# Moving three small bursts of matmuls in a hand-timed order: two steps of the fourth scan, and one projection of the decode tokens

## The chip, the cores and the metric

The kernel runs on one core of one Trainium2 chip. The metric is the device time of one execution in microseconds (us): three runs of the kernel before gave a median of 995.23 us (995.17 to 996.35). About 0.2%, or 2 us, is the least that a measurement of this kernel can tell from no change.

Five engines matter. TensorE (PE) multiplies matrices, VectorE (DVE) and ScalarE (ACT) work element by element, GpSimd (POOL) and SyncE (SP) mostly issue transfers. Each engine runs its own list of instructions in order and waits on semaphores for the others.

## The reference

One layer of a hybrid decoder step for one prompt of 2048 tokens and 8 decode tokens. The input is RMS-normalised and multiplied by a 1024 x 4096 matrix into eight groups of 512 columns: queries, keys, values and a gate for four retention heads, and query, forget gate, value and gate for four HGRN2 heads. Each head runs a decayed recurrence over the tokens:

```
o_inter = einsum('bhtd,bhdv->bhtv', qc * exp(b), S)          # b: cumulated log of the forget gate
A  = einsum('bhtd,bhsd,bhtsd->bhts', qc, kc, decay)           # HGRN2: the decay is per channel
o  = o_inter + einsum('bhts,bhsv->bhtv', A, vc)
S' = exp(bC) * S + einsum('bhsd,bhsv->bhdv', kc * exp(bC - b), vc)
```

Then comes a head-wise RMS norm, a SiLU gate, the output projection (1024 x 1024), the residual and a last RMS norm. Outputs are y for prompt and decode tokens and the final states.

## The kernel before, in words

**Units and products.** The input projection is cut into 24 units (`u` = 0 to 23, 12 for each half of the tokens); units 24 to 31 are the output projection. Unit `u` makes two rows of 128 columns for 1024 tokens: `u % 3` is 0 for HGRN2's forget gate and query (H in tile names), 1 for the two gates (G), 2 for retention's key and query (R). Each unit is a 2 x 2 block multiplication done with seven block products (`SLOTS`, line 876), each of 12 matmuls of 128 x 512: four blocks of the inner dimension by three terms of a high/low split. A product has a place in a time axis of 7 steps to a unit, and is issued in two halves of 6 matmuls. In a tile's name `aR`, `eR`, `bR` are the accumulators of a unit of kind R; `w11S` is a weight operand of unit 11, `x0T3h` the high part of the token operand T3 of the first half.

**The order is written out by hand.** `at(pos, f)` puts a function on a heap under a position; `after(d, f)` puts one `d` later than the function that is running. When everything is set up, the heap is emptied in order of position, and each function emits its instructions to all engines. So the position of an event sets the order on every engine at once, and nothing re-sorts it afterwards. The table `AT` holds the positions.

**The scan of an HGRN2 head** (`hgrn_rec`, line 1202) builds the 128 x 128 causal score blocks of eight chunks level by level. Each level needs k and q scaled by other products of forget gates. Its events for unit `u` stand at `7 u + AT["hgrn"][n] + AT["hd"][u // 3][n]`. There are eight scans, of units 0, 3, 6, ... 21; the second is that of unit 3, the fourth that of unit 9.

- First to third step, `s0`, `s1`, `s2` (`scores0`, `scores(1)`, `scores(3)`): a burst of 64 small matmuls by 32 x 16 (`small`, line 1269; the profile has two records for each), then on DVE `update` (kh and qth, lines 1234 and 1237), two masked copies (line 1275), and 0.35 later on ACT `keep` (copies of kh and qth, lines 1248 and 1249); 1.1 later another `update`. The change's title calls `s2` the second step and `s3` the third, counting from `s0` as zero.
- `s3` (`scores3`): two groups of small matmuls into the tiles p5 and p6 (lines 1321, 1330; both `plh` in the profile), a last `update`, and 0.3 later ten ACT copies into the score blocks `A`: four that read p5 (line 1340), two that read p6 (line 1342), four from `Ab` (line 1346).
- `k` (`kt`, line 1081): eight transposes of kh on TensorE (`pkh`, line 1085) into two tiles, and ACT copies of them (line 1091).

The small results of scans share one PSUM tag, `lv`, with two buffers (line 196), taken in turn: pl of `s1`, pl of `s2`, p5, p6, then the two tiles of the transposes. A new tile waits until all readers of the tile that had its buffer are done.

**The decode tokens.** For units 0 to 11, `dec_mm(u)` (line 804) multiplies the eight decode tokens with the raw weights of the unit (16 matmuls, `pdp`, line 809); `dec_copy` copies the result out on ACT. For a unit with `u % 3 == 0`, `dec_mm` stood at `7 u - 3.92`, for unit 3 just behind `s2` of the first scan.

**Next to the fourth scan** the token operands change from the first half to the second: `x_hi` on ACT (line 743) and `x_lo` on DVE (line 747) split what was loaded (`x1T1` and others), in two pieces each. `finish_block` of kind R rotates a block: two ACT copies (lines 1009, 1010, into `sw` or `big`) and three DVE operations (lines 1013, 1014, 750).

Of the kernel before, what the change touches and what calls it, by code (L numbers as in the profile page):

```python
# [48 lines left out]
def spooled(u):  # L49
    return u % 3 != 1 and u % 12 != 11  # L50
# [3 lines left out]
AT = {'wvl': (0.55, 0.6, 6.2, 6.6),  # L54
 's2': (0.4, 2.6),
 'vd': (9.4, 11.2),
 'hgrn': {'s0': 12.1,
          's1': 15.8,
          's2': 17.6,
          'load': 17.5,  # L60
          's3': 19.7,
          'k': 20.9,
# [79 lines left out]
         'fin': 25.2},  # L142
 'dh': ((12.15, 14.75), (17.55, 20.15), (27.15, 28.65)),
 'dhs': (-5.0, -2.2, -2.2, -1.5),
 'hd': ((0.0, 0.0, 0.0, 0.0), (0.0, 0.0, -0.5, -0.5), (0.0, 0.0, 0.0, 0.0), (0.3, 0.0, 0.0, 0.0),
        (0.0, 0.0, 0.0, 0.0), (0.0, 0.5, 0.0, 0.0), (0.0, 0.0, 0.0, 0.0), (0.0, 0.0, 0.0, 0.5)),
 'retL': {'load': 12.0,
          's': 11.55,
# [37 lines left out]
def step_kernel(ctx, tc, a, out):  # L186
# [31 lines left out]
    def at(pos, f):  # L218
        count[0] += 1
        heapq.heappush(ev, (pos, count[0], f))  # L220
# [550 lines left out]
    def w_load(u, n):  # L771
        R[u, n] = t_get([P, GW], f"r{u}{n}")
        row, kh = {"A11": (0, 0), "S3": (1, 0), "A22": (1, 1), "A12": (0, 1)}[n]
        sp.dma_start(R[u, n].rearrange("p (k t) -> p k t", k=4), w_src(u, row, kh))

    def w_s1(u):
        R[u, "S1"] = t_get([P, GW], f"r{u}S1")
        w_add(u, "S1", "S3", "A22", ALU.add)

    def w_s3(u):  # L780
        w_add(u, "S3", "A11", "S3", ALU.subtract)

    def w_s2(u):
        R[u, "S2"] = t_get([P, GW], f"r{u}S2")
        w_add(u, "S2", "A22", "S3", ALU.subtract)

    def w_s4(u):
        R[u, "S4"] = t_get([P, GW], f"r{u}S4")
        w_add(u, "S4", "A12", "S2", ALU.subtract)

    def w_split(u, n):
        w = W[u, n] = r_get(f"w{u}{n}")
        split_raw(w, R[u, n])
        t_done(R[u, n])
        if u < 12 and spooled(u):
            after(AT["late"], lambda: pool.dma_start(w_dram[u][W_NAMES.index(n)], w.bitcast(F32)))

    def w_reload(u, n):
        w = W[u, n] = r_get(f"w{u}{n}")
        sp.dma_start(w.bitcast(F32), w_dram[u - 12][W_NAMES.index(n)])  # L800
# [3 lines left out]
    def dec_mm(u):  # L804
        dec["pt"] = ps_o.tile([P, P], F32, tag="o", name=f"pdp{u}")
        for j in range(4):
            for g, n in enumerate(("A11", "A12", "S3", "A22")):
                at_ = 32 * (4 * (g % 2) + j)
                pe.matmul(
                    dec["pt"][32 * g : 32 * g + 32], xz[:, at_ : at_ + 32], R[u, n][:, j * P : (j + 1) * P],  # L810
                    start=(j == 0), stop=(j == 3),
                )

    def dec_copy(u):
        dec["e"] = t_get([P, P], f"de{u}")
        act.activation(dec["e"], dec["pt"], AF.Copy)

    def dec_sel(u):
        pt = ps_o.tile([P, 2, NB], F32, tag="o", name=f"pds{u}")
        pe.matmul(pt, dec["e"], sel16, start=True, stop=True)  # L820
        t_done(dec["e"])
        act.activation(draw[:, u % 3, :, u // 3], pt, AF.Copy)

    def prep_events(u):
        U = 7 * u
        w, d = AT["w"], AT["dec"]
        if 12 <= u < 24 and spooled(u):
            for name in W_NAMES:
                at(U + AT["re"][name], lambda name=name: w_reload(u, name))
            return  # L830
        for n, name in enumerate(("A11", "S3", "A22", "A12")):
            at(U + {0: -7.6, 1: -8.6}.get(u, AT["w24"][0] if u == 24 else w["load"] if u % 3 or u >= 12 else w["load0"]) + 0.5 * n, lambda name=name: w_load(u, name))
        if u < 12:
            if u == 3:
                at(AT["hgrn"]["s2"] + AT["hd"][0][2] + 0.01, lambda: dec_mm(u))
            else:
                at(U + d["mm" if u % 3 or not u else "mm0"], lambda: dec_mm(u))
            at(U + (-0.65 if u < 2 else d["copy" if u % 3 else "copy0"]), lambda: dec_copy(u))
            at(U + d["sel"], lambda: dec_sel(u))
        if u == 24:  # L840
            w = dict(w, **dict(zip(("S1", "S3", "S2", "S4"), AT["w24"][1:])))
        at(U + w["S1"], lambda: w_s1(u))
        at(U + w["S3"], lambda: w_s3(u))
        at(U + w["A11"], lambda: w_split(u, "A11"))
        at(U + w["S2"], lambda: w_s2(u))
        at(U + w["sS1"], lambda: w_split(u, "S1"))
        at(U + w["S4"], lambda: w_s4(u))
        at(U + w["sS2"], lambda: w_split(u, "S2"))
        at(U + w["sS4"], lambda: w_split(u, "S4"))
        at(U + w["sA12"], lambda: w_split(u, "A12"))  # L850
        at(U + w["sS3"], lambda: w_split(u, "S3"))
        at(U + w["sA22"], lambda: w_split(u, "A22"))
# [923 lines left out]
    for u in range(-6, 32):  # L1776
        U = 7 * u
        if u >= 0:
            prep_events(u)
        if 0 <= u < 24:  # L1780
            at(U - 0.01, lambda u=u: u_open(u))
        for n, sl in enumerate(SLOTS):
            s, d = sl[0], 0.5
            if is_last(u, n):
                s, d = (6.6, 0.2) if u < 0 else (7, 0.5)
            at(U + s, lambda u=u, n=n: product(u, n, 0))
            if u == 31 and is_last(u, n):
                at(U + s + 0.01, lambda u=u, n=n: evac(u, n))
            at(U + s + d, lambda u=u, n=n: product(u, n, 1))
            at(U + s + d + 0.01, lambda u=u, n=n: evac(u, n))  # L1790
# [164 lines left out]
```

## Time and profile before

| what | value |
|---|---|
| median of three runs | 995.23 us |
| the profiled execution | 994.56 us |
| its span from first to last instruction | 992.8 us |
| PE busy / DVE busy / ACT busy / POOL busy | 99% / 79% / 58% / 25% |
| granted TensorE clock | 0.999 |

In rows of the timeline the columns are: start from the span's beginning in us, time taken in us, engine, line, operation, output<-inputs, shapes, number of instructions merged into the row, and in brackets the idle time of the engine before it and what ended it. "issue" is idle time that no semaphore in the profile explains. A matmul's start is recorded and its end is modelled, so times on TensorE are best read from start to start. SP and POOL carry transfers; queue q8 carries instructions.

### The profile page before, as it was taken

The page shows a single profiled execution, that of the slowest core. Times are in us where ns is not written, and L with a number is a line of the kernel's source. Part 1 is how long each engine was busy: PE and PEld are TensorE (multiplying, and loading weights), DVE is VectorE, ACT ScalarE, POOL GpSimd, SP SyncE. Part 2 cuts the span into 40 slices and gives each one's busy share as a digit, 9 for nine tenths or more (in the row PEclk, how much of TensorE's full clock was granted, in tenths as well). Part 3 has the DMA queues.
Part 4 walks back from the last instruction along what each step waited for, and adds up shares of the span by engine and source line. Part 5 has one row for each costly group of instructions (what it writes and reads, how often), then busy time and mean ns, then how long its engine had stood idle before and what let it go on. Part 6 is the DMA issues. An engine that isn't in the chain of part 4 may idle for free. (4 is left out here: it accounts for less than half of the span.)

```text
span 992.8 us, 22960 instructions
## 1 busy us (share of the span) xinstructions
PE 978.9 (99%) x8831; PEld 815.9 (82%) x8831; DVE 779.6 (79%) x1355; ACT 575.5 (58%) x1348; POOL 252.5 (25%) x404
## 2 busy tenths in 40 slices
PE   9999999999999999999999999999999999999997
PEld 7788888888878887888888888888888878878886
DVE  6967696888778888878898766877867799867774
ACT  7855524856656664765885555456467577524332
POOL 1421231111332342232022222222237202312121
PEclk9999999999999999999999999999999999999999
DMA  9756669748868987784986993994996497784522
GB/s 310 239 182 245 223 218 360 291 154 301 261 194 279 300 284 266 269 273 159 354 277 187 320 307 121 317 303 130 317 333 215 156 362 275 244 267 156 212 85 85
DMA packets 121820, 244.05 MB, mean 246 GB/s; under 512 B 12600, under 2 KB 53184, under 8 KB 119024
## 3 DMA queue, kind: packets, MB, share of 16 engines
q1 hardware_dynamic: 98544, 164.69, 50.9%
q0 software_dynamic: 22880, 77.65, 21.1%
q8 instruction: 69, 1.13, 0.5%
q14 instruction: 39, 0.32, 0.1%
q10 hardware_dynamic: 288, 0.27, 0.1%
HBM read 155.97 MB, written 89.72 MB: 247 GB/s over the span
## 5 line engine op out<-in xcount | busy, mean ns | idle before, releaser
L1248 ACT ACTIVATE qh<-kh 128x1024 f32<-128x1024 f32 x24 | 25.5, 1062 | 46.3 <-DVE kh L1234 46.2
L1671 ACT ACTIVATE yj<-xro 128x512 f32<-128x512 f32 (+1 forms) x25 | 15.6, 624 | 60.3 <-DVE xro L750 42.7
L1234 DVE TENSOR_TENSOR kh<-kh,fph 128x512 f32<-128x512 f32 x48 | 33.0, 687 | 13.6 <-PE plh L1269 10.9
L1128 ACT ACTIVATE obh<-poh 128x128 f32<-128x128 f32 x64 | 16.9, 290 | 29.3 <-PE poh L1124 29.3
L1237 DVE TENSOR_TENSOR qth<-qth,fph 128x512 f32<-128x512 f32 x48 | 32.8, 683 | 0.0
L1128 ACT ACTIVATE obr<-por 128x128 f32<-128x128 f32 x64 | 16.8, 276 | 27.1 <-PE por L1124 27.1
L373 POOL TENSOR_TENSOR ms<-ms 128x2 f32<-128x2 f32 x8 | 10.0, 1255 | 86.5 <-ACT xn L369 86.5
L1689 DVE SCALAR_TENSOR_TENSOR xro<-xro,yms,fg 128x1024 f32<-128x1024 f32 (+1 forms) x16 | 20.0, 1247 | 13.5 <-POOL yms L1686 13.5
L1152 POOL DMA_DIRECT2D o_dram<-gtr x16 | 12.3, 769 | 67.5 <-DVE gtr L1149 20.8
L948 ACT ACTIVATE vo<-aV 128x512 f32<-128x512 f32 x12 | 7.1, 589 | 37.7 <-PE aV L918 37.7
L750 DVE TENSOR_TENSOR xro<-aO,xro 128x512 f32<-128x512 f32 (+1 forms) x33 | 22.2, 676 | 7.2 <-PE aO L918 7.1
L1152 POOL DMA_DIRECT2D o_dram<-gth x16 | 12.5, 778 | 57.5 <-DVE gth L1149 15.9
L265 POOL TENSOR_SCALAR orsh<-omsh 128x4 f32<-128x4 f32 x16 | 5.6, 347 | 83.3 <-ACT obh L1128 82.9
L1136 ACT ACTIVATE obh<-poh,orsh 128x128 f32<-128x128 f32 x64 | 18.2, 370 | 14.2 <-POOL orsh L266 14.2
L1115 DVE SCALAR_TENSOR_TENSOR sth<-sth,fph,puh 128x128 f32<-128x128 f32 x48 | 16.7, 347 | 10.3 <-PE poh L1124 7.8
L1122 PE MATMUL poh<-vh,A 128*128 128x128 f32 x128 | 24.0, 274 | 0.0
L1122 PE MATMUL por<-vr,A 128*128 128x128 f32 x128 | 24.0, 274 | 0.0
L1002 POOL DMA_DIRECT2D g_dram<-g x29 | 15.8, 546 | 27.8 <-DVE g L998 25.6
L1124 PE MATMUL por<-str,qr 128*128 128x128 f32 x112 | 21.8, 276 | 0.3 <-DVE str L1113 0.3
L369 ACT ACTIVATE xn<-xn 128x512 f32<-128x512 f32 x32 | 19.8, 622 | 3.5 <-DMA xn<-in_x_prompt 3.5
L1136 ACT ACTIVATE obr<-por,orsr 128x128 f32<-128x128 f32 x64 | 18.2, 368 | 6.1 <-POOL orsr L266 6.1
L1124 PE MATMUL poh<-sth,qth 128*128 128x128 f32 x112 | 21.7, 275 | 0.0
(1727 smaller groups left out, 3716.7 us busy)
## 6 DMA issues: line engine op xcount, KB each, us to landing
xn<-in_x_prompt SPq DMA_DIRECT2D x32, 256.0 KB, 4.4
v_dram<-vo SPq DMA_DIRECT2D x32, 256.0 KB, 2.4
xro<-in_x_prompt SPq DMA_DIRECT2D x16, 512.0 KB, 5.1
out_y_prompt<-xro POOLq DMA_DIRECT2D x15, 512.0 KB, 4.0
g_dram<-g POOLq DMA_DIRECT2D x29, 256.0 KB, 5.8
xr<-in_x_t SPq DMA_DIRECT2D x12, 512.0 KB, 6.2
vh<-v_dram SPq DMA_DIRECT2D x16, 256.0 KB, 8.8
gth<-g_dram SPq DMA_DIRECT2D x16, 256.0 KB, 6.7
```

The lines of the kernel that those rows point to most:

```text
L369: act.activation(r, r, AF.Square, accum_out=ms[:, 2 * h + j : 2 * h + j + 1])
L750: dve.tensor_tensor(o, x, y, op=ALU.add)
L1115: dve.scalar_tensor_tensor(dst, src, decay(c), pu[:, j], op0=ALU.mult, op1=ALU.add)
L1122: pe.matmul(po[:, j], s_ctx["A"][:, c], box["v"][g][:, j], start=True, stop=src is None)
L1124: pe.matmul(po[:, j], qcol(c), src, start=False, stop=True)
L1128: act.activation(ob[:, j], po[:, j], AF.Square, accum_out=ms[:, j : j + 1])
L1136: act.activation(ob[:, j], po[:, j], AF.Copy, scale=rs[:, j : j + 1])
L1152: after(AT["gate"]["tr"], lambda: pool.dma_start(o_dram[c0 : c0 + 4, ty, :, h].rearrange("c p t -> p c t"), gt.rearrange("p (c t) -> p c t ...
L1234: dve.tensor_tensor(kv[:, :, 0, :], kv[:, :, 0, :], two[:, :, 1:2].to_broadcast([P, nb, b]), op=ALU.mult)
L1237: dve.tensor_tensor(qv[:, :, 1, :], qv[:, :, 1, :], two[:, :, 0:1].to_broadcast([P, nb, b]), op=ALU.mult)
L1248: act.activation(kept_k, k, AF.Copy)
L1689: dve.scalar_tensor_tensor(x[:, cc], x[:, cc], ms[:, 0:1], fg[:, cc], op0=ALU.mult, op1=ALU.mult)
```

## The change

Three positions move. The second step (`s2`) of the fourth scan comes 1.0 later, its third (`s3`) 0.6 later, and `dec_mm` of unit 6 moves from 38.08 to 38.11, where `s2` of the second scan stands at 38.10. No instruction of computation is added or taken away; one wait instruction of TensorE (of 157) is no longer needed.

```diff
- 'hd': ((0.0, 0.0, 0.0, 0.0), (0.0, 0.0, -0.5, -0.5), (0.0, 0.0, 0.0, 0.0), (0.3, 0.0, 0.0, 0.0),
+ 'hd': ((0.0, 0.0, 0.0, 0.0), (0.0, 0.0, -0.5, -0.5), (0.0, 0.0, 0.0, 0.0), (0.3, 0.0, 1.0, 0.6),
         (0.0, 0.0, 0.0, 0.0), (0.0, 0.5, 0.0, 0.0), (0.0, 0.0, 0.0, 0.0), (0.0, 0.0, 0.0, 0.5)),
...
-            if u == 3:
-                at(AT["hgrn"]["s2"] + AT["hd"][0][2] + 0.01, lambda: dec_mm(u))
+            if u in (3, 6):
+                at(7 * (u - 3) + AT["hgrn"]["s2"] + AT["hd"][u // 3 - 1][2] + 0.01, lambda: dec_mm(u))
```

**Second scan, TensorE.** Before, from the last two `pdp` matmuls of unit 6 to the next product:

```order
L809 MATMUL pdp_3397<-r6S_3252,xz 32x128
L809 MATMUL pdp_3397<-r6A_3271,xz 32x128
L1269 MATMUL plh_3414<-fh_2585,qh_2625 32x16 x32
L1269 MATMUL plh_3414<-qth_2963,kh_2824 32x16 x32
L918 MATMUL aR_3234<-x0T2h,w5S_3231 128x512
```

Now, from the last matmul of the half product ahead to the first two of the 16 `pdp`:

```order
L918 MATMUL aR_3234<-x0T2h,w5S_3231 128x512
L1269 MATMUL plh_3397<-fh_2585,qh_2625 32x16 x32
L1269 MATMUL plh_3397<-qth_2963,kh_2824 32x16 x32
L809 MATMUL pdp_3464<-r6A_3241,xz 32x128
L809 MATMUL pdp_3464<-r6A_3282,xz 32x128
```

The two bursts, of 16 and 64 matmuls, have changed places; what stands before and behind them is the same.

**Fourth scan, TensorE, second step.** Before, at the end of product T2 of unit 11 (`aR`) and the start of product B22 (`eR`):

```order
L918 MATMUL aR_5391<-x0T2l,w11S_5388 128x512
L918 MATMUL aR_5391<-x0T2h,w11S_5388 128x512
L1269 MATMUL plh_5570<-fh_4744,qh_4783 32x16 x32
L1269 MATMUL plh_5570<-qth_5117,kh_4983 32x16 x32
L918 MATMUL eR_5419<-x0B22h,w11S_5416 128x512
```

Now, at the end of B22 and the start of B21 (`bR`):

```order
L918 MATMUL eR_5419<-x0B22l,w11S_5416 128x512
L918 MATMUL eR_5419<-x0B22h,w11S_5416 128x512
L1269 MATMUL plh_5586<-fh_4744,qh_4783 32x16 x32
L1269 MATMUL plh_5586<-qth_5117,kh_4983 32x16 x32
L918 MATMUL bR_5660<-x0B21h,w11A_5511 128x512
```

The burst has moved behind one product of 12 matmuls. In the same way p5 and p6, which stood between products B21 and T3 of unit 11, now stand in the middle of T3, 6 matmuls later; the transposes `pkh` keep their place behind T3, so 6 matmuls instead of 12 lie between p6 and them.

**Fourth scan, ACT.** Before, from the copy of qth that `keep` makes to the copies of the transposes:

```order
L1249 ACTIVATE fh_4744<-qth_5117 128x512
L1009 ACTIVATE sw_5676<-kr_5406 64x512
L1010 ACTIVATE sw_5676<-kr_5406 64x512
L743 ACTIVATE x1T1h<-x1T1l 128x1024
L1340 ACTIVATE A<-plh_5681 32x4x32 x4
L1342 ACTIVATE A<-plh_5682 64x4x64 x2
L1346 ACTIVATE A<-fh_4744 32x8x32 x4
L743 ACTIVATE x1T1h<-x1T1l 128x1024
L1009 ACTIVATE big<-kr_5406 64x512
L1010 ACTIVATE big<-kr_5406 64x512
L1091 ACTIVATE ksh_5762<-pkh_5757 128x512
```

Now:

```order
L1249 ACTIVATE fh_4744<-qth_5117 128x512
L1009 ACTIVATE sw_5674<-kr_5406 64x512
L1010 ACTIVATE sw_5674<-kr_5406 64x512
L743 ACTIVATE x1T1h<-x1T1l 128x1024 x2
L1009 ACTIVATE big<-kr_5406 64x512
L1010 ACTIVATE big<-kr_5406 64x512
L1340 ACTIVATE A<-plh_5692 32x4x32 x4
L1342 ACTIVATE A<-plh_5693 64x4x64 x2
L1346 ACTIVATE A<-fh_4744 32x8x32 x4
L1091 ACTIVATE ksh_5762<-pkh_5757 128x512
```

The ten copies into `A` now stand behind the second piece of `x1T1h` and a pair of rotation copies. On DVE the two additions into `kr` (from `eR` and from `bR`) now stand ahead of the scan's two updates instead of behind them. The orders of POOL and of SP are unchanged.

## Prediction

> **What bounds the kernel now.** I read the page first, then the waits of TensorE, then the timelines of the two stages that the change touches.
>
> ```profile
> span 992.8 us, 22960 instructions
> PE 978.9 (99%) x8831; PEld 815.9 (82%) x8831; DVE 779.6 (79%) x1355; ACT 575.5 (58%) x1348; POOL 252.5 (25%) x404
> ...
> PEclk9999999999999999999999999999999999999999
> ...
> q8 instruction: 69, 1.13, 0.5%
> ...
> PE plh L1269 <- issue: 3.4, 2, 2.5
> ```
>
> TensorE is busy from end to end at full clock, so the time is its list of instructions plus the holes in it. It waits 992.8 - 978.9 = 13.9 us in all; the largest single hole, 2.5 us, is inside a small burst and was ended by no semaphore ("issue"). An edit that moves bursts can save or cost time only by what a burst costs between products, and by holes.
>
> In the fourth scan before, TensorE has no hole:
>
> ```profile
> 475.01 0.39 PE L918 MATMUL aR<-x0T2h,w11S 128*128 128x512 f32 x1
> 475.33 0.70 PE L1269 MATMUL plh<-fh,qh 128*32 128x16 f32 x62
> ...
> 475.90 0.70 PE L1269 MATMUL plh<-qth,kh 128*32 128x16 f32 x62
> 476.53 0.50 PE L918 MATMUL eR<-x0B22h,w11S 128*128 128x512 f32 x1
> ...
> 479.18 0.39 PE L918 MATMUL eR<-x0B22h,w11S 128*128 128x512 f32 x1
> ...
> 481.90 0.39 PE L918 MATMUL bR<-x0B21h,w11A 128*128 128x512 f32 x1
> 482.22 0.46 PE L1321 MATMUL plh<-fh,qh 128*32 128x32 f32 x32
> 482.49 0.68 PE L1330 MATMUL plh<-qth,kh 128*32 128x64 f32 x32
> ...
> 485.97 1.03 PE L1085 MATMUL pkh<-ident,kh 128*128 128x128 f32 x8
> 486.76 0.48 PE L918 MATMUL aH<-x1B11h,w12A 128*128 128x512 f32 x1
> ```
>
> The last matmul of `eR` and that of `bR` are (481.90 - 479.18) / 12 = 0.227 us apart for each matmul. The burst of the second step takes 476.53 - 475.01 = 1.52 from product to product. The transposes (485.97) start with no gap.
>
> ACT in the same stretch:
>
> ```profile
> 478.90 1.06 ACT L1248 ACTIVATE qh<-kh 128x1024 f32<-128x1024 f32 x1 [2.04 <-DVE kh L1234]
> 479.86 0.61 ACT L1249 ACTIVATE fh<-qth 128x512 f32<-128x512 f32 x1
> ...
> 481.27 0.63 ACT L1010 ACTIVATE sw<-kr 64x512 f32<-64x512 f32 x1
> 481.93 1.06 ACT L743 ACTIVATE x1T1h<-x1T1l 128x1024 fp32r<-128x1024 f32 x1
> 482.89 1.09 ACT L1340 ACTIVATE A<-plh 32x128 f32<-32x128 f32 x4
> 484.00 0.77 ACT L1342 ACTIVATE A<-plh 64x256 f32<-64x256 f32 x2
> ...
> 486.38 1.06 ACT L743 ACTIVATE x1T1h<-x1T1l 128x1024 fp32r<-128x1024 f32 x1
> 487.47 0.63 ACT L1009 ACTIVATE big<-kr 64x512 f32<-64x512 f32 x1
> ```
>
> ACT goes from one instruction to the next here. The four copies that free p5's buffer end at 482.89 + 1.09 = 483.98, the two that free p6's at 484.77. The transposes, which take these two buffers, come 1.2 us later. That margin is what the change uses up.
>
> **The change part by part.** *Fourth scan, cost of the bursts themselves.* The 1.52 us for the second step are the same behind `eR` as behind `aR`, since on both sides stand matmuls of one shape; so are those of p5 and p6 inside a product. Term: 0.
>
> *Fourth scan, the ACT queue.* What is late next is worked out along the queues:
>
> - TensorE: `eR` now starts right behind 475.01; its last matmul starts at 475.01 + 12 x 0.227 = 477.73. The burst ends as before 0.07 after the next product's first start (475.90 + 0.70 = 476.60 against 476.53): 477.73 + 1.52 + 0.07 = 479.32.
> - DVE: `update` must wait for the burst, which reads kh. Before, DVE itself was late:
>
> ```profile
> 475.91 2.35 DVE L747 TENSOR_TENSOR x1B11l<-x1B11l,x1B11h 128x1024 fp32r<-128x1024 f32 x2
> 478.18 0.68 DVE L1234 TENSOR_TENSOR kh<-kh,fph 128x512 f32<-128x512 f32 x1
> 478.78 0.68 DVE L1237 TENSOR_TENSOR qth<-qth,fph 128x512 f32<-128x512 f32 x1
> ...
> 482.32 0.69 DVE L750 TENSOR_TENSOR kr<-bR,kr 128x512 f32<-128x512 f32 x1 [0.53 <-PE bR L918]
> ```
>
>   The addition from `eR`, now ahead, fits between 478.18 and 478.78. kh then runs from 479.32 + 0.05 (my value for a semaphore's way, between 0.03 from `bR`'s modelled end, 481.90 + 0.39, to 482.32, and 0.07) to 480.06, and ACT's first copy starts 0.04 after it (as 478.90 after 478.86): 480.10, or 1.20 later than before.
> - ACT, now with the second piece of `x1T1h` and a rotation pair ahead: 480.10 + 0.96 (L1248 to L1249) + 0.61 + 0.64 + 0.66 (the pair) + 0.96 (first piece) + 1.09 (second, 486.38 to 487.47) + 0.64 + 0.66 (second pair) = 486.32. The copies of p5 end 1.09 later, 487.41; those of p6 start 1.11 later and end at 487.43 + 0.77 = 488.20.
> - TensorE: the first four transposes, due at 485.97, wait until 487.46, the last four until 488.25. Four of eight take (486.76 - 485.97) / 2 = 0.40, so unit 12's product starts at 488.65 instead of 486.76: **+1.89 us**.
>
> Queued behind the waiting transposes is all that TensorE has left, and nothing takes the delay back: DVE, ACT and the loads of unit 12 keep their distance from TensorE, and no hole in this stretch is there to be used up.
>
> A smaller wait hides in it: p6 needs the second `update`, which now stands on DVE behind the addition from `bR` (482.32). kh and qth follow at 0.60 each and end at about 484.20, while p6 is due at 482.49 + 6 x 0.227 = 483.85. These 0.4 us would count if the transposes were free; as they are not, they cost nothing.
>
> The bounds of the 1.89: if ACT's chain started no later than before, it would be 0.69; the release can't come before its copies, and a late instruction block (below) in p6 adds up to 1.0. I take 1.89, since each duration is of the same instruction in the same place.
>
> *Second scan, the price of the pair.* `pdp` ahead of the burst is there before, the other order in the first scan:
>
> ```profile
> 306.13 0.39 PE L918 MATMUL aR<-x0T2h,w5S 128*128 128x512 f32 x1
> 306.45 0.30 PE L809 MATMUL pdp<-r6A,xz 128*32 128x128 f32 x2
> ...
> 308.90 0.39 PE L918 MATMUL aR<-x0T2l,w5S 128*128 128x512 f32 x1
> ...
> 222.88 0.39 PE L918 MATMUL aR<-x0T2h,w2S 128*128 128x512 f32 x1
> ...
> 225.63 0.40 PE L918 MATMUL eR<-x0B22l,w2S 128*128 128x512 f32 x1
> ...
> 322.96 0.29 PE L820 MATMUL pds<-pk,de 128*128 128x16 f32 x2
> ```
>
> From the last matmul ahead to the second behind: 2.77 against 2.75, so -0.02 us. The burst comes 0.9 us earlier, and what waits for it on DVE too; TensorE has no wait there that this could shorten. `pdp` itself ends some 1.1 us later, and its result is read on TensorE only at 322.96 (`pds`), so that costs nothing.
>
> *Second scan, the instruction block.* 17662 matmuls and weight loads to 69 transfers on q8 are 256 instructions to a transfer. The holes that end by "issue" lie a whole number of such blocks apart:
>
> ```profile
> 394.81 0.44 PE L1269 MATMUL plh<-qth,kh 128*32 128x16 f32 x31 [2.46 <-issue]
> ...
> 290.32:394.81 104.49, 102.04 (x1274) 85.66 (x1274) 87.99 (x161) 62.51 (x149) 33.31 (x56) 1.00 0.81 271
> 290.32:307.58 17.26, 17.26 (x256) 14.12 (x255) 16.00 (x32) 10.09 (x19) 5.70 (x10) 1.00 0.70 234
> 306.45:307.58 1.13, 1.13 (x60) 1.13 (x59) 0.48 (x1) 0.52 (x1) 0.00 (x0) 1.00 1.06 409
> 475.33:475.86 0.53, 0.53 (x63) 0.53 (x64) 0.53 (x1) 0.53 (x2) 0.00 (x0) 1.00 1.10 382
> ...
> q8 instruction: 1, 0.02, 6.2%
> ```
>
> Between the hole at 290.32 and that at 394.81 lie 2548 instructions and some semaphore waits: ten blocks. The block that ended the second hole came in at 392.53 to 393.56 (the last row is the queue's in that window; 6.2% of 16 engines is one engine all the time), so work went on 1.25 us after its landing. Two blocks behind 290.32 the list crosses into another block at 307.58, 60 instruction pairs into the pair of bursts. That block landed at 305.88 (304.91 to 305.88 gives the same queue row), so it is usable at 307.13 or a little later: before, no hole. Now the larger burst leads, and 60 pairs of it take about 0.50 us (63 in 0.53), so the crossing is due at 306.95: a hole of 0.2 to 0.4. The bounds are 0 (the block lands 0.2 earlier) and about 0.5; I take +0.28, the middle of what the rows give.
>
> The Trainium skill ("Runtime: NRT & Kernel Launch", Instruction fetch mechanics) says that instructions come in blocks of 256 and that crossing a block is mostly hidden, as the sequencer is slower than the refill. The block size agrees with the rows; the holes at 290.32 and 394.81 show that small bursts outrun the refill. By that rule this term would be 0.
>
> *Sum.* 994.56 (the profiled execution) + 1.89 - 0.02 + 0.28 = 996.71. The median lies 0.67 above that execution; with it 995.23 + 2.15 = 997.38. I say **997.3 us**, 0.2% slower.
>
> **The rivals.**
>
> 1. *The block is hidden in the second scan.* Only the ACT queue counts: +1.87, 997.1, just under the 0.2% line of 997.2. For it: 0.2 us is little, and a landing that comes 0.3 earlier does it. Against: the landing is of a request made long before the change. Chance 0.20. The page of the Trainium skill named above ("Runtime: NRT & Kernel Launch") would have it so.
> 2. *The copies don't hold the transposes*: ACT reaches them sooner, because the pieces of `x1T1h` and the rotation run while it waits, and only p6's 0.4 us and the block's 0.28 show: 995.9. For it: ACT idled 2.04 before 478.90. Against: all these stand behind `qh<-kh` in its list, so they can't use that time. Chance 0.11.
> 3. *Not slower: the hole at 394.81 closes.* With TensorE 0.3 us later in front of the third scan's bursts, the request of that block would get in ahead of the transfers it queues with; it decides from about 2.5 us earlier. Price -2.64 (the hole and its restart): 994.7. Against: nothing of the change acts on those transfers. Chance 0.09.
> 4. *One more late block*, in p6 or in a later burst, since all of them meet other transfers now: a hole of 1.0 (the difference between usual and late ones is 1 to 2.6): 998.3. Chance 0.10.
>
> That the orders move as the diff says is plain from the rows of the orders, so that is no rival.
>
> **How the numbers follow.** The forecast has 0.50, with a range of its own from 996.9 to 997.8. The range of 8 in 10 leaves out most of rival 3 and the far end of rival 4: 995.4 to 998.4. A change under 0.2% can't be told from none. Slower by more: 0.40 of the forecast's 0.50 (it lies only 0.1 above the line), 0.03 of rival 1, 0.09 of rival 4, so 0.52. Faster by more: 0.05, the part of rival 3 in which TensorE also waits less for the copies. The rest, 0.43, is no change.
>
> **What would show it.** Right: `pkh` in the fourth scan starts at about 487.5 on the clock of before, with a wait of about 1.5 us ended by ACT's A (L1340) and another of 0.4 by L1342; ACT runs L743 twice, then L1009, L1010, L1340; a hole by "issue" of 0.2 to 0.4 in the second scan's `plh`. Wrong: `pkh` without a wait, L1340 before 485, or a total within 1 us of before.

## The result, and the profile after

| | before | after |
|---|---|---|
| median of the runs timed side by side | 995.20 us | 997.73 us |
| ratio after to before, 95% interval | | 1.0021 (1.0011 to 1.0031) |
| the profiled execution, its span | 994.56, 992.8 us | 997.31, 995.5 us |

The change makes the kernel slower by about 2.1 us (1.1 to 3.1). The prediction was 997.3 us, with "slower" as the likeliest side.

The page of the changed kernel, and the waits of TensorE there (in the waits: us in total, how often, the longest):

```profile
span 995.5 us, 22959 instructions
PE 979.9 (98%) x8831; PEld 816.1 (82%) x8831; DVE 780.0 (78%) x1355; ACT 575.7 (58%) x1348; POOL 249.4 (25%) x404
...
PE plh L1269 <- issue: 3.2, 2, 2.1
PE bG L918 <- issue: 1.3, 1, 1.3
...
PE pkh L1085 <- ACT A L1340: 0.8, 1, 0.8
...
PE plh L1330 <- issue: 0.4, 1, 0.4
...
PE plh L1330 <- DVE qth L1237: 0.3, 1, 0.3
```

Two of these waits are for ACT and DVE and are not among TensorE's waits before: `pkh` for ACT's A, and `plh` of L1330 (p6) for DVE's qth. Here they are on TensorE, in the fourth scan:

```profile
477.65 0.39 PE L918 MATMUL eR<-x0B22h,w11S 128*128 128x512 f32 x1
...
483.49 0.46 PE L1321 MATMUL plh<-fh,qh 128*32 128x32 f32 x32
484.27 0.76 PE L1330 MATMUL plh<-qth,kh 128*32 128x64 f32 x32 [0.33 <-DVE qth L1237]
...
487.40 1.45 PE L1085 MATMUL pkh<-ident,kh 128*128 128x128 f32 x8 [0.77 <-ACT A L1340]
488.61 0.49 PE L918 MATMUL aH<-x1B11h,w12A 128*128 128x512 f32 x1
```

and on ACT:

```profile
480.01 1.06 ACT L1248 ACTIVATE qh<-kh 128x1024 f32<-128x1024 f32 x1 [3.24 <-DVE kh L1234]
...
482.92 2.01 ACT L743 ACTIVATE x1T1h<-x1T1l 128x1024 fp32r<-128x1024 f32 x2
484.95 0.63 ACT L1009 ACTIVATE big<-kr 64x512 f32<-64x512 f32 x1
...
486.24 1.10 ACT L1340 ACTIVATE A<-plh 32x128 f32<-32x128 f32 x4
487.37 0.77 ACT L1342 ACTIVATE A<-plh 64x256 f32<-64x256 f32 x2
```

Both pieces of `x1T1h` and a second rotation pair now stand ahead of L1340. The first four transposes start 0.06 after these copies end (486.24 + 1.10 = 487.34); the last four wait for the copies of L1342 as well, which is why the row of eight is 1.45 long, and not 1.03 as before. The loads of the transposes' weights (PEld) show the two waits apart:

```profile
487.40 0.42 PEld L1085 LDWEIGHTS pkh<-ident,kh 128*128 128x128 f32 x4 [1.20 <-ACT A L1340]
488.19 0.42 PEld L1085 LDWEIGHTS pkh<-ident,kh 128*128 128x128 f32 x4 [0.37 <-ACT A L1342]
```

From the large matmul ahead to the second one behind, less two plain steps of 0.227, p5 and p6 cost 1.68 us (1.08 before) and the transposes 2.23 (0.89 before): 0.60 + 1.35 = 1.95 us more.

In the second scan, where the burst now leads the pair:

```profile
305.85 0.39 PE L918 MATMUL aR<-x0T2h,w5S 128*128 128x512 f32 x1
306.17 0.74 PE L1269 MATMUL plh<-fh,qh 128*32 128x16 f32 x64
306.74 0.71 PE L1269 MATMUL plh<-qth,kh 128*32 128x16 f32 x62
...
308.63 0.40 PE L918 MATMUL aR<-x0T2l,w5S 128*128 128x512 f32 x1
```

There is no hole by issue in it: 308.63 - 305.85 = 2.78, against 2.77 before. The spans differ by 2.7 us. 1.95 of them are the fourth scan; of the rest, 0.4 is the new issue wait of L1330 (it is in the seventh scan, at 727.56), and what is left is spread in small pieces.

### The profile page after: what moved, and what is told of

Its sections match the earlier page's. It is cut to its first block, busy times and chain, and to the rows that moved or that the text cites. A ratio compares the mean times of both kernels' runs of the same rounds, so it can differ in the third digit from the quotient of the medians.

```text
span 995.5 us, 22959 instructions
## 1 busy us (share of the span) xinstructions
PE 979.9 (98%) x8831; PEld 816.1 (82%) x8831; DVE 780.0 (78%) x1355; ACT 575.7 (58%) x1348; POOL 249.4 (25%) x404
## 5 line engine op out<-in xcount | busy, mean ns | idle before, releaser
L373 POOL TENSOR_TENSOR ms<-ms 128x2 f32<-128x2 f32 x8 | 5.7, 709 | 88.6 <-ACT xn L369 88.6
L1152 POOL DMA_DIRECT2D o_dram<-gtr x16 | 12.3, 768 | 61.8 <-DVE g L998 27.5
```

The lines of the kernel that those rows point to most:

```text
L1152: after(AT["gate"]["tr"], lambda: pool.dma_start(o_dram[c0 : c0 + 4, ty, :, h].rearrange("c p t -> p c t"), gt.rearrange("p (c t) -> p c t ...
```

## The experiments

Each ratio is to the runs of the kernel before on the same chip; us are worked out as the ratio by the median of before there.

### The half of the change in the second scan

```diff
-            if u == 3:
-                at(AT["hgrn"]["s2"] + AT["hd"][0][2] + 0.01, lambda: dec_mm(u))
+            if u in (3, 6):
+                at(7 * (u - 3) + AT["hgrn"]["s2"] + AT["hd"][u // 3 - 1][2] + 0.01, lambda: dec_mm(u))
```

> Only the second half of the change: pdp of unit 6 behind the second scan's second step; the fourth scan stays as before. Theory A (the whole difference comes from the fourth scan's copies, and the instruction block of the second scan lands in time): the pair of pdp and burst costs 2.32 us between the large matmuls around it, as in both kernels; unit 12's pkh has no wait above 0.1 us; no difference, within 0.2 us of before. Theory B (the late block of my prediction): a hole ended by issue of 0.2 to 0.4 us in plh of the second scan, and 0.28 us more. Theory C (the hole at 727.56 us of the changed kernel, 0.66 us, is brought on by this move and not by the scatter of transfers): it stands in the seventh scan's third step here too.

Measured: 0.9998 (0.9983 to 1.0012), -0.2 us. The transposes of unit 12 cost 0.89 us as before, and the hole at 727.56 is not there, nor in the two kernels below that have this move too, so theory C is out. But this profile has a hole where theory B puts it:

```profile
307.50 0.21 PE L1269 MATMUL plh<-fh,qh 128*32 128x16 f32 x3 [0.46 <-issue]
```

It makes the pair 0.62 us dearer than without it. The other profiles of this study that run this pair at the same block boundary say what it is. With the burst ahead, the hole at the crossing adds 0 (the change), 0.62 (here), 0.36 and 0.66 (two kernels below). With `pdp` ahead it adds 0 four times, 0.25 and 0.30. So the hole comes in both orders, from one execution to the next. The means, 0.41 and 0.09, lie 0.3 apart, about the term of the prediction, but ten profiles with such a scatter do not settle that, and the timing, with an interval of about 1.4 us to each side, cannot see it.

### The half of the change in the fourth scan

```diff
- 'hd': (... (0.3, 0.0, 0.0, 0.0),
+ 'hd': (... (0.3, 0.0, 1.0, 0.6),
```

> Only the first half of the change: the fourth scan's second step one product later and its third 0.6 of a product; pdp of unit 6 stays where it was. Theory A (ACT's copies into A, behind the second x1T1h piece and a rotation pair, hold the transposes of unit 12): pkh<-ident,kh waits 0.77 us on A of L1340 and again on L1342, p6 waits 0.33 us on DVE's qth; the transposes and the bursts of p5 and p6 cost 1.95 us more than before between the large matmuls around them, and the time is 1.9 us (1.5 to 2.5) above before. Theory B (the waits in the trace are made up elsewhere, and the difference of the whole change comes from instruction blocks): 0.5 us or less above before.

Measured: 1.0017 (1.0004 to 1.0030), +1.7 us. TensorE in the fourth scan:

```profile
484.75 0.71 PE L1330 MATMUL plh<-qth,kh 128*32 128x64 f32 x32 [0.33 <-DVE qth L1237]
...
487.87 1.45 PE L1085 MATMUL pkh<-ident,kh 128*128 128x128 f32 x8 [0.83 <-ACT A L1340]
```

The same two waits as in the changed kernel. By the steps between large matmuls they cost 0.55 + 1.40 = 1.95 us. Theory A holds: in the trace this half has the whole cost of the change's fourth scan, and the timing agrees (1.7, 0.4 to 3.0, against 2.1).

### The copies into A ahead in ACT's list

The whole change with one number different, which leaves TensorE's list as in the changed kernel and moves only what stands around the ten copies on ACT:

```diff
- 'hd': (... (0.3, 0.0, 1.0, 0.6),
+ 'hd': (... (0.3, 0.0, 1.0, 0.45),
```

> The whole change, but with the fourth scan's third step 0.45 of a product later instead of 0.6: TensorE's order is that of the changed kernel, instruction for instruction; on ACT the copies of p5 and p6 into A (L1340, L1342) now stand ahead of the second x1T1h piece and the rotation pair behind it. Theory A (the place of these copies in ACT's list is the cause): pkh's wait falls from 0.77 us to 0.1 or less, its cost between the large matmuls around it from 2.23 to 0.9 us; what stays is p6's wait for qth on DVE, 0.3 to 0.6 us; the time is 0.3 to 0.7 us above before and 1.3 us (1.0 to 1.6) below the changed kernel. Theory B (the second step's later place on TensorE costs by itself, whatever ACT does): the time stays 1.9 us above before.

Measured: 1.0002 (0.9988 to 1.0015), +0.2 us. ACT, where one piece of `x1T1h` and not two with a rotation pair stands ahead of the copies:

```profile
481.98 1.06 ACT L743 ACTIVATE x1T1h<-x1T1l 128x1024 fp32r<-128x1024 f32 x1
483.09 1.10 ACT L1340 ACTIVATE A<-plh 32x128 f32<-32x128 f32 x4
484.22 0.77 ACT L1342 ACTIVATE A<-plh 64x256 f32<-64x256 f32 x2
```

and TensorE:

```profile
483.35 0.69 PE L1330 MATMUL plh<-qth,kh 128*32 128x64 f32 x32 [0.33 <-DVE qth L1237]
485.46 1.03 PE L1085 MATMUL pkh<-ident,kh 128*128 128x128 f32 x8
```

The transposes no longer wait and cost 0.89 us, and p6's wait costs 0.53, as theory A has it. TensorE runs the same list in both kernels, so it is the place of the copies on ACT that costs the change 1.35 us at the transposes.

### Only the third step later

```diff
- 'hd': (... (0.3, 0.0, 0.0, 0.0),
+ 'hd': (... (0.3, 0.0, 0.0, 0.6),
```

> The fourth scan's second step is back in its old place, and only the third is 0.6 of a product later: ACT's copies stand behind the second x1T1h piece and the rotation pair, as in the changed kernel, but the chain that brings qh to ACT begins as early as before. Theory A (the prediction's two parts of the delay: 0.69 us from the place in ACT's list, 1.20 us from the later start of the chain): pkh waits on A of L1340 and L1342, the first transposes start about 1.2 us earlier than in the changed kernel, and the time is 0.7 us (0.4 to 1.0) above before. Theory B (the list alone decides, since ACT has no slack to use up): 1.9 us above before. Theory C (the late start alone decides): no wait, 0.2 us or less above before.

Measured: 1.0008 (0.9994 to 1.0023), +0.8 us, whose interval alone would not exclude zero. ACT, and TensorE behind it:

```profile
479.83 1.06 ACT L1248 ACTIVATE qh<-kh 128x1024 f32<-128x1024 f32 x1 [2.04 <-DVE kh L1234]
...
481.57 0.63 ACT L1009 ACTIVATE sw<-kr 64x512 f32<-64x512 f32 x1 [0.16 <-DVE kr L750]
...
486.20 1.10 ACT L1340 ACTIVATE A<-plh 32x128 f32<-32x128 f32 x4
```

```profile
487.36 1.46 PE L1085 MATMUL pkh<-ident,kh 128*128 128x128 f32 x8 [0.32 <-ACT A L1340]
```

The transposes cost 1.80 us, 0.91 more than before. My bound for this case was 0.69; the 0.16 that ACT waits for DVE's `kr`, here as in the kernel before, is most of what I had left out. So the two parts of the delay are both real: 0.91 from the place in ACT's list, and the rest of the 1.95 from the chain that starts 1.2 us later.

### The update ahead on DVE

As with the copies ahead, and besides:

```diff
-            after(1.1, lambda: update(li))
+            after(0.85 if u == 9 and li == 5 else 1.1, lambda: update(li))
```

> As the kernel with the fourth scan's third step 0.45 later (copies ahead), and besides the second update of that scan is issued ahead of the addition from bR on DVE. Theory A (with both orders put right the later second step costs TensorE nothing): p6 has no wait for qth, the bursts of p5 and p6 cost 1.08 us between the large matmuls around them instead of 1.61, pkh has no wait, and the time is that of before within 0.3 us, 0.5 us below the kernel with the copies ahead. Theory B (the addition from bR, now behind the update, holds a buffer of bR or the third step): a new wait of 0.3 us or more on L918 or in p5, and the time 0.3 to 0.8 us above before.

Measured: 1.0014 (1.0001 to 1.0027), +1.4 us. p6's wait is gone (p5 and p6 cost 1.08), but the transposes wait after all, now for DVE:

```profile
483.49 0.68 PE L1330 MATMUL plh<-qth,kh 128*32 128x64 f32 x32
485.99 1.06 PE L1085 MATMUL pkh<-ident,kh 128*128 128x128 f32 x8 [0.24 <-DVE kh L1234]
```

```profile
484.02 1.23 DVE L747 TENSOR_TENSOR x1T1l<-x1T1l,x1T1h 128x1024 fp32r<-128x1024 f32 x1 [1.01 <-ACT x1T1h L743]
485.16 0.69 DVE L1234 TENSOR_TENSOR kh<-kh,fph 128x512 f32<-128x512 f32 x1
```

They cost 1.32, 0.43 more than before, against the 0.53 saved at p6. Behind p6's wait stood the next one: the last `update` waits on DVE behind a subtraction that waits for ACT's `x1T1h`. Neither theory had that; both took DVE's list behind p6 for free. So in the trace of the fourth scan the edit is worth 0.10 us, and what it leaves is 0.43 above before. Where the rest of the timed 1.4 comes from is not shown. Its interval overlaps that of the kernel with the copies ahead (0.2, -1.2 to 1.5), and the profiled execution, with four issue holes in `plh` (4.1 us in all, against two with 3.4 before), one of them, 1.22 us at 712.44, in a place where no other profile has one, stands for itself alone.

### The same move in the third scan

The largest hole of before, in the third scan, offers a test of the blocks of 256 instructions: the move puts 24 slow entries ahead of the boundary in place of 24 fast ones.

```diff
- 'hd': (... (0.0, 0.0, 0.0, 0.0), (0.3, 0.0, 0.0, 0.0),
+ 'hd': (... (0.0, 0.0, 1.0, 0.45), (0.3, 0.0, 0.0, 0.0),
...
-            after(1.1, lambda: update(li))
+            after(0.5 if u == 6 and li == 5 else 1.1, lambda: update(li))
```

> The kernel before, with the same move made in the third scan instead: its second step one product later, its third 0.45, its second update ahead on DVE. The crossing into another block of 256 instructions, at which TensorE has its longest hole (2.64 us at 394.81, ended by issue), then comes some 2.5 us later in time, since 24 instructions of a product (2.7 us) go ahead of it in place of 24 of the burst (0.2 us). Theory A (the hole is a block that lands late, and its request comes at a fixed place far ahead in the list): the hole falls below 0.5 us; the time is 2.3 us (1.6 to 2.8) below before, less up to 0.4 us for waits in p6. Theory B (the request moves along with the burst, or the hole belongs to the burst itself): a hole by issue of 2 us or more stays in that burst, and the time is that of before within 0.4 us.

Measured: 0.9985 (0.9972 to 0.9997), -1.5 us, median 993.79 against 995.59. The second half of the burst, and the window that held the hole before (busy time of each engine, granted clock, DMA share, GB/s):

```profile
395.09 0.70 PE L1269 MATMUL plh<-qth,kh 128*32 128x16 f32 x62
```

```profile
391.00:396.00 5.00, 5.00 (x145) 4.08 (x144) 1.36 (x4) 0.77 (x2) 1.31 (x2) 1.00 1.03 405
```

TensorE is busy throughout, where before it was for 2.54 of these 5 us. The hole (2.46 us of waiting, 2.64 with the restart) is gone; `pkh` waits for DVE's kh instead, which ends at 402.53, 0.84 after ACT's copies have freed p5's buffer, and costs 0.29 more. The timed gain is 1.5 (0.3 to 2.8). Theory A holds, though its 2.3 came from a single execution: in the seven profiles that have this hole TensorE waits 1.36 to 2.46 us in it, 1.9 in the mean, and the kernel before has the longest. 1.9 less 0.29 is near the timed gain. This kernel beats both the kernel before and the changed one. It is the change's own move, in a scan where TensorE had a hole for it to fill.

### The eighth scan too

```diff
-        (0.0, 0.0, 0.0, 0.0), (0.0, 0.5, 0.0, 0.0), (0.0, 0.0, 0.0, 0.0), (0.0, 0.0, 0.0, 0.5)),
+        (0.0, 0.0, 0.0, 0.0), (0.0, 0.5, 0.0, 0.0), (0.0, 0.0, 0.0, 0.0), (0.0, 0.0, 1.0, 0.5)),
...
-            after(0.5 if u == 6 and li == 5 else 1.1, lambda: update(li))
+            after({6: 0.5, 21: 0.85}.get(u, 1.1) if li == 5 else 1.1, lambda: update(li))
```

> As the kernel with the move in the third scan, and the same in the eighth: its second step one product later, its third 0.5, its second update ahead on DVE. Theory A (blocks that land late): the hole of 1.16 us at 799.7 falls below 0.4 us too, and the time is 3.0 us (2.0 to 4.0) below before. Theory B (the hole belongs to the burst): it stays, and the time is that of the kernel with the third scan alone. Theory C (eighth scan: a wait on DVE or ACT takes the hole's place): no hole by issue, but waits of 0.5 us or more behind it, and 0 to 0.5 us of gain over the third scan alone.

Measured: 0.9990 (0.9975 to 1.0006), -1.0 us. The eighth scan's hole is gone, but p6 waits there for DVE, whose chain is late for a load:

```profile
806.59 0.65 PE L1330 MATMUL plh<-qth,kh 128*32 128x64 f32 x32 [1.79 <-DVE qth L1237]
```

```profile
801.09 0.69 DVE L762 TENSOR_TENSOR r24S<-r24S,r24A 128x512 f32<-128x512 f32 x1 [1.15 <-DMA r24A<-o_dram]
...
804.55 0.69 DVE L309 TENSOR_TENSOR w24A<-r24A,w24A 128x512 fp32r<-128x512 f32 x1 [0.43 <-ACT w24A L308]
```

That is theory C: one wait for another. I then tried to take the rounding of w24A out of the chain:

```diff
-            after({6: 0.5, 21: 0.85}.get(u, 1.1) if li == 5 else 1.1, lambda: update(li))
+            after({6: 0.5, 21: 0.5}.get(u, 1.1) if li == 5 else 1.1, lambda: update(li))
```

> The kernel with the move in the third and the eighth scan, with the eighth scan's second update one place further ahead on DVE (in front of the rounding of w24A, 0.60 us). Theory A (p6's wait of 1.99 us there is DVE's chain, whose rounding of w24A waits for ACT): qth ends 1.0 us earlier (the 0.60 and the 0.43 of waiting ahead of it), p6's wait falls to 0.9 us, and the time is 1.0 us (0.4 to 1.6) below the kernel without this. Theory B (the chain is late because of the load of r24A, 1.15 us of waiting ahead of the first kh, and the rounding only fills that time): p6 waits as before, no difference.

Measured: 0.9986 (0.9974 to 0.9998), -1.4 us, which the timing cannot tell from -1.0. TensorE's waits there (us in total, times, longest; each is a single wait, in the eighth scan):

```profile
PE plh L1330 <- DVE qth L1237: 1.0, 1, 1.0
PE pkh L1085 <- DVE kh L1234: 0.8, 1, 0.8
```

p6's wait fell from 1.8 to 1.0, as theory A has it, and `pkh` took up what p6 gave back: p5, p6 and the transposes cost 3.04 + 1.23 = 4.27 us without the edit, 2.32 + 1.90 = 4.21 with it. Theory A is right on p6, but of the 1.0 us that it foresaw the trace shows 0.06. Whether the load is why, as theory B has it, is not settled: the chain waits for r24A in both (1.15 and 1.56 us), but in this execution it lands 0.4 us later against TensorE's bursts, which is most of the 0.46 that the chain gained behind it.

### All block boundaries moved

```diff
- 'wu': 35,
+ 'wu': 51,
```

> The kernel before with 51 warm-up matmuls instead of 35 (their result is never read): 64 more entries in TensorE's list ahead of everything, so that every block boundary falls 64 entries earlier in the program; no order changes, and TensorE waits for the first loads in any case. Theory A (holes ended by issue belong to block boundaries): the holes at 290.3 (L918 bG) and 394.8 (plh) of before are gone; new ones of 1.5 to 4 us stand where boundaries now fall close behind one another, in the second scan's plh near 308 and in pah<-qth,kh near 457; the time is 4 us above before (0 to 9). Theory B (they belong to those bursts, their operands or a port): the holes stay on the same instructions and no new one appears; the time is that of before within 0.5 us.

Measured: 1.0124 (1.0095 to 1.0152), +12.3 us, from 64 more entries whose own cost is 0.7 us at the start (the first product begins at 5.91 instead of 5.20). The two instructions that had the large holes before, and the two places foreseen for new ones:

```profile
290.63 0.40 PE L918 MATMUL bG<-x0B21l,w4A 128*128 128x512 f32 x1
...
313.52 0.24 PE L1269 MATMUL plh<-qth,kh 128*32 128x16 f32 x5 [4.23 <-issue]
...
401.00 0.70 PE L1269 MATMUL plh<-qth,kh 128*32 128x16 f32 x62
...
466.72 0.25 PE L1269 MATMUL pah<-qth,kh 128*32 128x16 f32 x6 [2.75 <-issue]
```

The holes of before are closed and the new ones stand where they were foreseen (309.3 and 464.0, where these waits begin, are 308 and 457 of before plus the delay so far). Theory A holds for the places; theory B is out. The size was above my range, and the granted clock says why, for the most part. TensorE in windows around the two holes (busy us, granted clock, DMA share, GB/s):

```profile
309.00:313.60 4.60, 0.37 (x40) 1.00 0.81 315
313.60:317.70 4.10, 4.10 (x16) 0.58 0.16 54
...
463.70:466.80 3.10, 0.35 (x38) 1.00 0.14 32
466.80:472.00 5.20, 5.20 (x23) 0.67 0.01 3
```

After each of these holes TensorE ran for 4 to 5 us at 0.58 and 0.67 of its clock: 4.10 x 0.42 + 5.20 x 0.33 = 3.4 us on top of the holes. Two more holes of 1.5 us came in `bG` and `aG`, and a `pdp` waited 2.0 for its load. The issue holes of the whole kernel grew from 4.5 us to 9.9, which with 3.4, 2.0 and 0.7 makes 11.5 of the 13.7 by which the spans differ.

The other way, on top of the kernel with the third scan's move:

```diff
- 'wu': 35,
+ 'wu': 23,
```

> The kernel with the move in the third scan, and besides 23 warm-up matmuls instead of 35 (their result is never read): 48 fewer entries in TensorE's list ahead of everything, so that every block boundary falls 48 entries later in the program than there. Theory A (holes by issue belong to boundaries that follow too soon on the one before): in the kernel with the third scan's move two boundaries stand 2.3 us apart at 289.9, and there the hole of 1.71 us is; with the shift no two that matter stand closer than 5.9 us, counted from 48 entries ahead of the first. The hole at 289.9 goes and no other above 1.2 us comes; the time is 1.5 us (0.3 to 2.5) below the kernel with the third scan's move, 3 us below before. Theory B (that hole belongs to bG<-x0B21l,w4A, its weights or a port): it stays on that instruction, and the time is that of the kernel with the third scan's move within 0.5 us.

Measured: 1.0082 (1.0069 to 1.0096), +8.2 us, where I expected -3.

```profile
228.90 0.42 PE L809 MATMUL pdp<-r3A,xz 128*32 128x128 f32 x2 [4.64 <-issue]
...
295.70 0.40 PE L918 MATMUL bG<-x0B21l,w4A 128*128 128x512 f32 x1
```

```profile
223.90:228.90 5.00, 0.36 (x33) 0.80 1.00 340
228.90:234.00 5.10, 5.10 (x39) 0.53 0.59 216
```

The hole in `bG` is gone, so it belonged to the boundary and not to that instruction (theory B is out). But a block that I took for harmless came late: it was to be some 6.4 us behind the place in the list where I presumed its request, and the transfers filled all DMA engines in that window (share 1.00). A hole of 4.64 us, the slower clock behind it (5.10 x 0.47 = 2.4 us) and two more of 1.98 and 1.42 us in later bursts make the loss: the issue holes grew from 2.2 us in the kernel with the third scan's move to 8.4, which with 2.4 makes 8.6 of the 9.2 by which the spans differ. Which boundaries stand close together can be read from the list; how long a block then takes, I could not foresee.

## Why the prediction was right, point by point

- **What bounds the kernel.** Right: all that could be traced of the differences in these runs was waits of TensorE or its clock.
- **Fourth scan, the bursts themselves: 0.** Right: the second step's burst costs 1.40 us above the plain steps in both kernels.
- **Fourth scan, the ACT queue: +1.89.** Right, step by step. The last matmul ahead of the moved step, 475.01 before, is 0.08 earlier in this execution (the same number of steps back from 477.65 gives 474.93), so 0.08 is added to the times after. `qh`: predicted 480.10, measured 480.01 + 0.08 = 480.09. L1340: 486.32, measured 486.32. The transposes: 487.46, measured 487.48. Unit 12's product: 488.65, measured 488.69. That is 1.93 behind the 486.76 of before, and p5, p6 and the transposes cost 1.95 more. Of the signs, `pkh` was to wait about 1.5 by L1340 and 0.4 by L1342: its start is 1.51 later, of which p6's wait had already taken 0.60, and the second wait is 0.37. The half of the change with this part alone costs the same 1.95 and is 1.7 us slower (0.4 to 3.0).
- **p6's hidden wait, about 0.4.** Right in place, cause and in that it hides: DVE's second kh stands behind the addition from `bR`, and with the copies ahead the wait shows by itself, at 0.53. What I did not see is that, with p6's wait removed, the last `update` is next in line behind it, at 0.43.
- **The lower bound of 0.69** (the chain starts as early as before) measured 0.91: it left out the 0.16 that ACT waits for DVE's `kr`, which the kernel before has as well.
- **Second scan, the pair: -0.02.** Measured: 0.01 more. Nothing either way.
- **Second scan, the instruction block: +0.28.** In the changed kernel's profile it is 0: the block's transfer there ran from 303.45 to 304.55, and not from 304.91 to 305.88, so work that came at 306.67 did not wait. That was rival 1's condition ("a landing that comes 0.3 earlier does it"). Against it I had held that the landing answers a request made before the change; the request may be, but the transfer starts 1.5 us earlier in this profile than in that of before, where TensorE itself is only 0.3 earlier. The right term is a spread, 0 to 0.66 with the burst ahead and 0 to 0.30 with `pdp` ahead, whose means lie 0.3 apart without being settled.
- **The page of the Trainium skill** ("Runtime: NRT & Kernel Launch", Instruction fetch mechanics), by which a crossing is mostly hidden, is right for this one crossing in that profile and not for the kernel: when 64 entries were put ahead, only the places of the crossings and a start 0.7 us later changed, and the time went up by 12.3 us.
- **The sum.** The trace has 1.95 for what was foreseen as 1.87 without the block. The medians of many runs give 2.1 (1.1 to 3.1), where 2.15 was foreseen with it. That these meet to 0.05 is luck: 0.28 of the 2.15 did not happen in this profile, and of the 2.7 us between the profiled spans 0.4 is the hole at 727.56 and another 0.35 was not traced. The sum also reads 997.38, which is nearer to 997.4 than to the 997.3 of the forecast.
- **The other rivals.** 2 (the copies don't hold the transposes) is out by the trace and by the kernel with the copies ahead. 3 (the hole at 394.81 closes) did not happen; it stands at 394.74 with 2.10 us of waiting. There was a price to be had: the move in the third scan, which brings the boundary 2.5 us later, closed it and made the kernel 1.5 us faster, not 2.64. 4 (one more late block) happened at a small size, 0.4 us at 727.56.

## What to carry to other kernels

When a burst moves later, follow the chain that it starts through each engine's list, entry by entry, up to the buffer that the next large piece of work needs: here that sum was right to 0.04 us in the profile, and a change of one number in the order (0.6 to 0.45) takes most of the loss away. A wait that is removed uncovers the next one in line, so the gain of an edit is bounded by the second latest release, not by the latest. And in this kernel a list with dense bursts of small instructions has a price that belongs to its position and to no line of it: entries added or taken at the start moved this kernel's time by 8 to 12 us.

## What the runs showed of the hardware that was not expected

A hole in TensorE's work can cost more than its length. After holes of 4.23, 4.64 and 2.75 us the granted clock was 0.58, 0.53 and 0.67 in the mean of the next 4 to 5 us, and in windows of 1 us inside these stretches it reads 0.50. After the hole of 2.46 us in the kernel before it stayed at 1.00 (busy us, granted clock, DMA share, GB/s):

```profile
396.00:404.00 8.00, 8.00 (x96) 1.00 0.59 207
```

So the time lost grows by a jump, somewhere between these lengths as far as four holes can show. The Trainium skill ("TensorE: Matmul & The Clock Gate", Part 1: The HAM clock gate) says that TensorE drops to half of its clock after an idle window of about 3.4 us, and needs a busy one to come back. The runs agree on the half clock, and on how long it lasts: worked out from the means of short windows, 3.4 us behind the holes of 4.23 and 2.75 (314.3 to 317.7, 467.9 to 471.3), and 6.8 us with the hole of 4.64, the last 4.8 of them behind it. A hole of 2.75 us, which was enough here, is shorter than the window that the page names.

The second is how late a block can come. In the profiles with the boundaries of before, holes by issue sum to 1.3 to 5.2 us; with the boundaries moved by 64 or 48 entries they sum to 9.9 and 8.4, one block alone costing 4.64 with the DMA engines full and another 2.75 with a DMA share of 0.14. The block's own transfer (the last one on q8 before work goes on) splits these holes. In those of 2.46, 2.75, 4.23 and 4.64 us it starts 0.2, 0.1, 1.7 and 2.1 us after TensorE ran out, takes 1.0, 1.3, 1.0 and 1.1, and work goes on 1.25, 1.4, 1.5 and 1.4 us after its end. So some 2.5 us go when the transfer starts only as TensorE runs out, and what makes the two longer holes longer is a later start. What sets the start of these transfers was not settled.
